# Attention in a hybrid decoder layer: the products of the turned probabilities with the values wait for both heads' copies

## The chip, the cores and the metric

The kernel runs on one core of one Trainium2 chip. The time is in device microseconds. Before the change three runs took 1358.27, 1357.81 and 1360.36 us; their median is 1358.27 us.

## The reference

One decoder layer on 1024 tokens of width 1024, all in float32. Cut to the part around the change:

```
q, k, v, iq, ik, iw, hq, hf, hi, hg = split(x @ w_in)
score = sum_h iw[t,h] * relu(iq[t,h] . ik[s])            # indexer, causal
keep the 256 best keys of each query                      # mask
s   = (q . k) * 64**-0.5, -inf where not kept             # 8 heads of 64
att = softmax(s) @ v
hgo = hgrn2(hq, hf, hi, hg)                                # 4 heads of 128, chunkwise
x   = LayerNorm(alpha * x + concat(att, hgo) @ w_o)
x   = LayerNorm(alpha * x + relu(x @ w_up)**2 @ w_down)
```

## The kernel before, in words

The layer is one program in stages: input projections with the choice of keys and the recurrent heads beside them, then attention, then the output projection with `w_o`, the first layer norm, and the two products of the feed-forward part. A scheduler of the language sets the order on each engine: it takes the instructions in the order in which the code issues them, with their dependencies, and lets an instruction go ahead of others on its engine by an estimate of when it is ready. So the written order is a wish, and the built order is read from the program.

Attention works on four pairs of heads (`hp`). Queries come in eight tiles of 128 (`t`), taken two at a time (`m` = 0, 2, 1, 3). For one query tile `scores` (L667) makes the products of queries and keys (L684, L685, in two parts of the keys) into one of four PSUM banks; VectorE adds the mask and takes the row maximum (L686), GpSimd scales it (L688), and ScalarE takes the exponent (L690) into the tiles `pr` or `prs`.

The probabilities have to be turned before they can meet the values. A unit of that is (`hp`, `m`, `c`): two query tiles, and the two key tiles 2c and 2c+1. `turn` (L694) does it for each of the two heads: four transposes on TensorE (L703; three where `c == m`, on the diagonal, since one of the four blocks is masked) into a PSUM bank of the tag `tr`, of which there are two, and a copy into `pt`: by VectorE for head 0, by ScalarE for head 1 (L710 and L712). `gather` (L715) makes the products with the values. A full unit (`c < m`) has four of them, head 0 and 1 for each of two key tiles, 256 columns each (L729). Head 0 writes the partitions 0 to 63 of the result, head 1 the partitions 64 to 127, so the page shows them as `128*64`: 128 rows by 64 columns of the array. A unit on the diagonal has two products of 128 columns (L731) and two of 256; the one at `m == 0` has six of 128 (L726, L727). There are ten units in a pair of heads and 40 in all.

The loop over `plan` (L763) issues the scores of a query tile and, between them, the turns of the pair of tiles before; the products run `LAG = 2` units behind the turns (L782). `normalise` (L741) closes half a pair: products with `ident` that spread the reciprocal sums (L744), a copy, a multiplication and the split into two parts.

`fetch` (L650) loads queries, keys and values of the next pair; the loads of the keys (`ks`) are issued only when an exponent of the pair before is done (L662). The four key loads of a head are two parts of the keys, each written twice, and L685 uses the second part. `w_o` follows: its weights are split into two parts (L88 on ScalarE, L89 on GpSimd) once the last exponent is done (L873), and its products (L123 to L125) fill the gaps in the last part of attention.

Of the kernel before, what the change touches and what calls it, by code (L numbers as in the profile page):

```python
# [13 lines left out]
AF = mybir.ActivationFunctionType  # L14
# [28 lines left out]
def layer(ctx, tc, x, w_in, w_o, lb_logits, hg_norm_g, ln1_g, ln1_b, w_up, w_down, ln2_g, ln2_b,  # L43
          rope_tab, turn_tab, ident_c, causal_c, level_c, block_c, out, probe=None):
    nc = tc.nc
    PE, ACT, DVE, POOL = nc.tensor, nc.scalar, nc.vector, nc.gpsimd
# [27 lines left out]
    def tr_bank(shape=(P, 4, P)):  # L74
        return bank("tr", 2, shape)

    def ou_bank(shape=(P, 512)):
        return bank("ou", 2, shape)
# [7 lines left out]
    def split_out(hi, lo, src, eng=None):  # L86

        first = ACT.activation(hi, src, AF.Copy)  # L88
        (eng or DVE).tensor_tensor(lo, src, hi.bitcast(F32), op=OP.subtract)  # L89
        return first  # L90

    def behind(a, b):
        tc.add_manual_dep(a.ins, b.ins.name, mybir.DependencyInfo(
            mybir.DependencyClass.Sync, mybir.DependencyReason.DATA), reason="order of the work")
# [496 lines left out]
    for at in range(1, 29):  # L591
        if at in groups:
            g = groups[at]()
# [50 lines left out]
    bp = es_b.enter_context(tc.tile_pool(name="bp", bufs=1, reuse_waits="tile"))  # L644
    scale = HD ** -0.5
    PB = 5, 4
    PT, LAG, FT = 8, 2, 1
    pairs, probs, parts = {}, {}, {}

    def fetch(hp, after=None):  # L650

        qs = bq.tile([P, 2, S], F32R, name="qs1") if hp % 2 else qp.tile([P, 2, S], F32R, name="qs")
        for j in range(2):
            dma(qs[j * HD:(j + 1) * HD].bitcast(F32), qd[j, 2 * hp:2 * hp + 2].rearrange("h x d s -> (x d) h s"))
        ks = []
        for hh in range(2):
            ks.append([wp.tile([P, S], F32R, name="ks", tag="w", bufs=9) for _ in range(2)])
            for j in range(2):
                for r in range(2):
                    d = dma(ks[hh][j][r * HD:(r + 1) * HD].bitcast(F32), kd[j, 2 * hp + hh].rearrange("x d s -> (x d) s"))  # L660
                    if after is not None:
                        behind(d, after)  # L662
        va = bq.tile([P, NT, P], F32, name="va1") if hp % 2 else bp.tile([P, NT, P], F32, name="va")
        dma(va, vd[:, hp * P:(hp + 1) * P].rearrange("(t p) n -> p t n", p=P))
        pairs[hp] = {"ks": ks, "qs": qs, "va": va}

    def scores(hp, t):  # L667
        ks, qs = pairs[hp]["ks"], pairs[hp]["qs"]
        W = P * (t + 1)
        mask = causal[:, P:] if t == 0 else causal if t == 1 else score[t - 2]  # L670
        cuts = 1 if W <= 512 else 2
        n = W // cuts
        if "sums" not in pairs[hp]:
            pairs[hp]["sums"] = bp.tile([P, NT, 2], F32, name="sums", bufs=2)
        sums = pairs[hp]["sums"][:, t]
        mx = bp.tile([P, 2, 2], F32, name="mx", bufs=4)
        nm = bp.tile([P, 2], F32, name="nm", bufs=4)
        pr = [bp.tile([P, S], F32, name="pr", bufs=PB[0]) if t > 3 else bp.tile([P, 512], F32, name="prs", bufs=PB[1])
              for _ in range(2)]
        for hh in range(2):  # L680
            for ci in range(cuts):
                c = slice(ci * n, (ci + 1) * n)
                ps = mm_bank()
                PE.matmul(ps[:, :n], qs[:, hh, t * P:(t + 1) * P], ks[hh][0][:, c], start=True, stop=False)  # L684
                PE.matmul(ps[:, :n], qs[:, hh, t * P:(t + 1) * P], ks[hh][1][:, c], start=False, stop=True)  # L685
                DVE.tensor_tensor_reduce(pr[hh][:, c], ps[:, :n], mask[:, c], 1.0, mx[:, 0, hh:hh + 1] if ci else -HUGE,  # L686
                                         op0=OP.add, op1=OP.max, accum_out=mx[:, ci, hh:hh + 1])
        POOL.tensor_scalar(nm, mx[:, cuts - 1], -scale, None, op0=OP.mult)  # L688
        for hh in range(2):
            pairs[hp]["last"] = ACT.activation(pr[hh][:, :W], pr[hh][:, :W], AF.Exp, bias=nm[:, hh:hh + 1],  # L690
                                               scale=scale, accum_out=sums[:, hh:hh + 1])
        probs[hp, t] = pr

    def turn(hp, m, c):  # L694

        parts[hp, m, c] = []
        for hh in range(2):
            pt = bp.tile([P, 2, 2, P], F32, name="pt", bufs=PT)
            tp = tr_bank((P, 2, 2, P))
            n = 4 if c < m else 3  # L700
            for i in range(2):
                for g in range(2 * c, 2 * c + 2 if c < m or i else 2 * c + 1):
                    PE.transpose(tp[:, g % 2, i], probs[hp, 2 * m + i][hh][:, g * P:(g + 1) * P], ident)  # L703
            if c < m:
                cp = [(pt.rearrange("p g t n -> p (g t n)"), tp.rearrange("p g t n -> p (g t n)"))]
            else:
                cp = [(pt[:, 0], tp[:, 0]), (pt[:, 1, 1], tp[:, 1, 1])]
            for d, u in cp:
                if hh:
                    ACT.activation(d, u, AF.Copy)  # L710
                else:
                    DVE.tensor_copy(d, u)  # L712
            parts[hp, m, c].append(pt)

    def gather(n, hp, m, c):  # L715
        half, i = divmod(2 * m, 4)
        if c == 0 and i == 0:
            pairs[hp]["o", half] = ou_bank((P, 4, P))
        o, va, pt = pairs[hp]["o", half], pairs[hp]["va"], parts.pop((hp, m, c))
        for g in (0, 1) if c < m else (1, 0):  # L720
            for hh in range(2):
                sl = slice(hh * HD, (hh + 1) * HD)
                lhs = va[:, 2 * c + g, sl]
                if m == 0:
                    if g == 1:
                        PE.matmul(o[sl, i], va[:, 0, sl], pt[hh][:, 0, 0], start=True, stop=True)  # L726
                    PE.matmul(o[sl, i + 1], lhs, pt[hh][:, g, 1], start=g == 1, stop=g == 0)  # L727
                elif c < m or g == 0:
                    PE.matmul(o[sl, i:i + 2], lhs, pt[hh][:, g], start=c == 0 and g == 0, stop=c == m)  # L729
                else:  # L730
                    PE.matmul(o[sl, i + 1], lhs, pt[hh][:, 1, 1], start=False, stop=False)  # L731
        if c == m and i == 2:
            sums = pairs[hp]["sums"][:, 4 * half:4 * half + 4]
            wide = bq.tile([P, 4, 2, HD], F32, name="wide")
            DVE.reciprocal(sums, sums)
            POOL.tensor_copy(wide, sums.unsqueeze(3).to_broadcast([P, 4, 2, HD]))
            late.append((n, hp, half, o, wide))

    late = []

    def normalise(due, hp, half, o, wide):  # L741
        ps = tr_bank()
        for i in range(4):
            PE.matmul(ps[:, i], wide[:, i].rearrange("p h d -> p (h d)"), ident, start=True, stop=True)  # L744
        r = bq.tile([P, 4, P], F32, name="recip")
        ACT.activation(r, ps, AF.Copy)
        DVE.tensor_tensor(r, o, r, op=OP.mult)
        split_out(MH[half][:, :, hp, :], ML[half][:, :, hp, :], r, POOL)
# [9 lines left out]
    turned_ = [p for p in plan if p[0] == "turn"]  # L758
    fetch(0)
    hgt = turn_hg()  # L760
    next(g1)
    nt = ns = 0
    for n, (kind, hp, *u) in enumerate(plan):  # L763
        if kind == "scores":
            scores(hp, *u)
            if ns < 4:
                next(hgt)
                next(hgt)
            if ns < 2:
                next(g1)  # L770
            if ns == 4:
                for _ in hgt:
                    pass
                es_h.close()
                bq = es_b.enter_context(tc.tile_pool(name="bq", bufs=1, reuse_waits="tile", side="right"))
            if (ns == 4 or ns > 8 and u[0] == FT) and hp < 3:
                fetch(hp + 1, pairs[hp]["last"])
            ns += 1
        else:
            turn(hp, *u)  # L780
            nt += 1
            if nt > LAG:  # L782
                gather(nt, *turned_[nt - 1 - LAG][1:])
                if late and late[0][0] + 2 <= nt:
                    normalise(*late.pop(0))
    for p in turned_[nt - LAG:]:
        gather(nt, *p[1:])
    for u in late:
        normalise(*u)
# [372 lines left out]
```

## Time and profile before

| | |
|---|---|
| median of three runs | 1358.27 us |
| the profiled execution: time, span of its instructions | 1360.36 us, 1358.1 us |
| PE (TensorE matmul) busy | 1308.9 us, 96% |
| DVE (VectorE), ACT (ScalarE), POOL (GpSimd) busy | 71%, 44%, 28% |
| attention, from the first to the last transpose of probabilities | 464.7 to 605.2 us |
| products with the values (L726 to L731) | to 611 us |

The trace counts two instructions for one product with the values: a run "x8" of L729 is four products. A transpose is counted once. A run is a row of equal instructions; its length is read as the time from its start to the start of the next row, since the pipeline lets the ends overlap. "PEld" is the load of the stationary operand.

### The profile page before, as it was taken

The page shows a single profiled execution, that of the slowest core. Times are in us where ns is not written, and L with a number is a line of the kernel's source. Part 1 is how long each engine was busy: PE and PEld are TensorE (multiplying, and loading weights), DVE is VectorE, ACT ScalarE, POOL GpSimd, SP SyncE. Part 2 cuts the span into 40 slices and gives each one's busy share as a digit, 9 for nine tenths or more (in the row PEclk, how much of TensorE's full clock was granted, in tenths as well). Part 3 has the DMA queues.
Part 4 walks back from the last instruction along what each step waited for, and adds up shares of the span by engine and source line. Part 5 has one row for each costly group of instructions (what it writes and reads, how often), then busy time and mean ns, then how long its engine had stood idle before and what let it go on. Part 6 is the DMA issues. An engine that isn't in the chain of part 4 may idle for free.

```text
span 1358.1 us, 21018 instructions
## 1 busy us (share of the span) xinstructions
PE 1308.9 (96%) x8007; PEld 1065.7 (78%) x8007; DVE 960.5 (71%) x1731; ACT 599.0 (44%) x1070; POOL 375.1 (28%) x374
## 2 busy tenths in 40 slices
PE   9999999799989999999989999999998999999996
PEld 8888788687879866668867888888886788888875
DVE  5576579999998555523487666656628999887478
ACT  3442457555432655542235555555544343333131
POOL 3452523535253111143480000000005342231016
PEclk9999999899999999999999999999999999999999
DMA  6333411202013564035223544444467555352223
GB/s 231 103 118 106 133 53 32 64 2 64 33 56 75 138 147 109 1 117 166 106 78 106 189 135 152 148 163 147 141 215 275 181 165 185 118 163 92 80 76 124
DMA packets 93620, 162.50 MB, mean 120 GB/s; under 512 B 6600, under 2 KB 37712, under 8 KB 93392
## 3 DMA queue, kind: packets, MB, share of 16 engines
q1 hardware_dynamic: 72880, 122.89, 28.9%
q10 hardware_dynamic: 20640, 38.28, 8.1%
q8 instruction: 63, 1.03, 0.3%
q14 instruction: 37, 0.30, 0.1%
HBM read 114.48 MB, written 46.66 MB: 119 GB/s over the span
## 4 chain that ended last, share of the span: by engine, by line
PE 67%; DVE 18%; DMA 6%; POOL 4%; issue 3%; ACT 1%; SPq 0%; DVEq 0%; POOLq 0%; ACTq 0%
PE ps L124 18%; PE ps L123 18%; PE ps L125 18%; DVE junk L322 6%; PE ps L729 3%; PE ps L703 3%; DMA qd<-rparts 2%; DMA kd<-rparts 2%; PE ps L684 2%; DVE hgk L492 1%; PE ps L685 1%; DVE hgq L491 1%; POOL tn L904 1%; POOL acc L830 1%; DVE pos L380 1%
## 5 line engine op out<-in xcount | busy, mean ns | idle before, releaser
L125 PE MATMUL ps<-w,xt 128*128 128x512 f32 (+2 forms) x448 | 157.7, 353 | 0.0
L124 PE MATMUL ps<-w,xt 128*128 128x512 f32 (+2 forms) x448 | 156.9, 352 | 0.0
L123 PE MATMUL ps<-tw,sh 128*128 128x512 f32 x392 | 152.8, 393 | 4.2 <-DVE acc L1068 2.4
L123 PE MATMUL ps<-w,xt 128*128 128x512 f32 (+2 forms) x448 | 156.0, 354 | 0.5 <-ACT xt L88 0.5
L124 PE MATMUL ps<-tw,sh 128*128 128x512 f32 x392 | 154.4, 394 | 1.9 <-DVE tw L89 1.9
L125 PE MATMUL ps<-tw,sh 128*128 128x512 f32 x392 | 153.1, 393 | 0.4 <-DVE sh L89 0.4
L89 POOL TENSOR_TENSOR w<-wraw,w 128x512 fp32r<-128x512 f32 (+1 forms) x76 | 102.4, 1368 | 108.8 <-ACT w L88 78.4
L1048 POOL TENSOR_TENSOR tt<-rb,rb 128x1536 f32<-128x1536 f32 (+1 forms) x5 | 18.4, 3677 | 390.9 <-PE ps L125 314.1
L1070 DVE TENSOR_TENSOR acc<-acc,ps 128x512 f32<-128x512 f32 x140 | 92.0, 678 | 35.4 <-PE ps L125 35.2
L88 ACT ACTIVATE sh<-rs 128x1536 fp32r<-128x1536 f32 (+1 forms) x35 | 49.1, 1403 | 151.7 <-PE ps L125 140.8
L123 PE MATMUL ps<-xt,w 128*128 128x512 f32 x256 | 102.9, 402 | 0.0
L322 DVE TENSOR_SCALAR_CACHE_REDUCE junk<-score,cand 128x384 uint8<-128x384 f32 (+1 forms) x124 | 100.4, 810 | 3.0
L125 PE MATMUL ps<-xt,w 128*128 128x512 f32 x256 | 102.2, 402 | 0.0
L124 PE MATMUL ps<-xt,w 128*128 128x512 f32 x256 | 101.8, 398 | 0.0
L124 PE MATMUL ps<-xt,wq 128*128 128x512 f32 x256 | 99.9, 390 | 0.0
L123 PE MATMUL ps<-xt,wq 128*128 128x512 f32 x256 | 99.7, 389 | 0.0
L125 PE MATMUL ps<-xt,wq 128*128 128x512 f32 x256 | 99.5, 390 | 0.0
L340 ACT ACTIVATE sjunk<-score,cand 128x896 int8<-128x896 f32 (+1 forms) x62 | 67.9, 1095 | 66.6 <-DVE cand L351 64.0
L123 PEld LDWEIGHTS ps<-w,xt 128*128 128x128 f32 x448 | 84.7, 190 | 11.6 <-ACT xt L88 1.0
L124 PEld LDWEIGHTS ps<-w,xt 128*128 128x128 f32 x448 | 84.9, 190 | 11.2 <-issue 1.3
L125 PEld LDWEIGHTS ps<-w,xt 128*128 128x128 f32 x448 | 85.0, 190 | 10.5 <-issue 0.4
L123 PEld LDWEIGHTS ps<-tw,sh 128*128 128x128 f32 x392 | 74.0, 189 | 20.8 <-DVE acc L1068 2.8
(242 smaller groups left out, 3063.6 us busy)
## 6 DMA issues: line engine op xcount, KB each, us to landing
hs<-h ACTq DMA_DIRECT2D x98, 256.0 KB
rs<-hs SPq DMA_DIRECT2D x28, 768.0 KB
wr<-in_w_up_dram SPq DMA_DIRECT2D x16, 1024.0 KB
rb<-in_w_down_dram SPq DMA_DIRECT2D x16, 768.0 KB
wraw<-in_w_in_dram SPq DMA_DIRECT2D x40, 256.0 KB
ks<-kd SPq DMA_DIRECT2D x32, 256.0 KB
xn<-in_x_dram SPq DMA_DIRECT2D x8, 512.0 KB
kd<-rparts ACTq DMA_DIRECT2D x16, 256.0 KB
```

What stands on the lines that cost most here:

```text
L88: first = ACT.activation(hi, src, AF.Copy)
L89: (eng or DVE).tensor_tensor(lo, src, hi.bitcast(F32), op=OP.subtract)
L123: PE.matmul(ps, ah, bh, start=first, stop=False, **kw)
L124: PE.matmul(ps, ah, bl, start=False, stop=False, **kw)
L125: return PE.matmul(ps, al, bh, start=False, stop=last, **kw)
L322: DVE.tensor_scalar(junk[:, :wide[j]], score[j], at, 0.0, op0=op, op1=OP.add, accum_out=res)
L340: ACT.activation(sjunk[:, :wide[j]], score[j], AF.Sign, bias=0.0 if at is None else at[:, j:j + 1], scale=1.0, accum_out=cnt[:, j:j + 1])
L684: PE.matmul(ps[:, :n], qs[:, hh, t * P:(t + 1) * P], ks[hh][0][:, c], start=True, stop=False)
L703: PE.transpose(tp[:, g % 2, i], probs[hp, 2 * m + i][hh][:, g * P:(g + 1) * P], ident)
L729: PE.matmul(o[sl, i:i + 2], lhs, pt[hh][:, g], start=c == 0 and g == 0, stop=c == m)
L1048: POOL.tensor_tensor(t1, b12, b11, op=OP.subtract)
L1070: DVE.tensor_tensor(acc[t][:, gs], acc[t][:, gs], ps, op=OP.add)
```

## The change

The copies of a unit are noted by head, and the first product of the unit gets a dependency on both of them, where it had one on its own head's copy alone. `BATCH = 1` gives one unit at a time. `normalise` is issued before the products of the step instead of behind them.

```
-    PT, LAG, FT = 8, 2, 1
-    pairs, probs, parts = {}, {}, {}
+    PT, LAG, BATCH, FT = 8, 2, 1, 1
+    pairs, probs, parts, copies, waited = {}, {}, {}, {}, []
...
-                if hh:
-                    ACT.activation(d, u, AF.Copy)
-                else:
-                    DVE.tensor_copy(d, u)
+                copy = ACT.activation(d, u, AF.Copy) if hh else DVE.tensor_copy(d, u)
+                copies[hp, m, c, hh] = copy
...
+    def values(r):
+
+        while waited:
+            behind(r, waited.pop())
...
-                    PE.matmul(o[sl, i:i + 2], lhs, pt[hh][:, g], start=c == 0 and g == 0, stop=c == m)
+                    values(PE.matmul(o[sl, i:i + 2], lhs, pt[hh][:, g], start=c == 0 and g == 0, stop=c == m))
...
-            if nt > LAG:
-                gather(nt, *turned_[nt - 1 - LAG][1:])
-                if late and late[0][0] + 2 <= nt:
-                    normalise(*late.pop(0))
-    for p in turned_[nt - LAG:]:
+            if late and late[0][0] + 2 <= nt:
+                normalise(*late.pop(0))
+            if nt - LAG - gathered >= BATCH:
+                batch = turned_[gathered:nt - LAG]
+                waited += [copies[(*p[1:], hh)] for p in batch for hh in range(2)]
+                for p in batch:
+                    gather(nt, *p[1:])
+                gathered += len(batch)
+    for p in turned_[gathered:]:
         gather(nt, *p[1:])
```

`values` wraps the other first products (L726, L731) in the same way. The new lines move the numbers: L729, L731, L744 and L747 of the kernel before are L732, L734, L747 and L750 of the changed one, and L726 and L727 are L729 and L730.

On TensorE, in the second pair of heads, the three full units of `m == 3` that have no scores between them (`ident` marks transposes, `pt,va` products with the values) stood so:

```order
L703 MATMUL ps<-ident,pr 128x128 x4
L729 MATMUL ps<-pt,va_5270 64x256
L703 MATMUL ps<-ident,pr 128x128 x4
L729 MATMUL ps<-pt,va_5270 64x256 x3
L703 MATMUL ps<-ident,pr 128x128 x4
L729 MATMUL ps<-pt,va_5270 64x256
L703 MATMUL ps<-ident,pr 128x128 x4
L729 MATMUL ps<-pt,va_5270 64x256 x3
L703 MATMUL ps<-ident,pr 128x128 x3
L729 MATMUL ps<-pt,va_5270 64x256
L703 MATMUL ps<-ident,pr 128x128 x3
L729 MATMUL ps<-pt,va_5270 64x256 x3
```

One product of a unit stood between the transposes of the two heads, and three behind them. On the same engine, at the same place, the changed program has:

```order
L703 MATMUL ps<-ident,pr 128x128 x8
L732 MATMUL ps<-pt,va_5270 64x256 x4
L703 MATMUL ps<-ident,pr 128x128 x8
L732 MATMUL ps<-pt,va_5270 64x256 x4
L703 MATMUL ps<-ident,pr 128x128 x6
L732 MATMUL ps<-pt,va_5270 64x256 x4
```

The single product has moved behind the second head's transposes and stands with the other three; the transposes of both heads stand together.

On TensorE, at the first scores of the second pair, with the semaphores that each instruction waits for (`DMAHW` are DMA queues; `qs_5255` is the second pair's queries), the kernel before has:

```order
L703 MATMUL ps<-ident,prs 128x128 [waits DVE_49]
L703 MATMUL ps<-ident,prs 128x128 x2
L729 MATMUL ps<-pt,va 64x256
L685 MATMUL ps<-ks,qs_5255 128x128 [waits DMAHW3_49,DMAHW2_49]
L684 MATMUL ps<-ks,qs_5255 128x256 [waits DVE_49]
L685 MATMUL ps<-ks,qs_5255 128x256
L703 MATMUL ps<-ident,prs 128x128 [waits Activation_49]
L703 MATMUL ps<-ident,prs 128x128 x2
L729 MATMUL ps<-pt,va 64x256 x3
```

On the same engine the changed program has there:

```order
L685 MATMUL ps<-ks,qs_5255 128x128 [waits DMAHW3_49,DMAHW2_49]
L703 MATMUL ps<-ident,prs 128x128 [waits DVE_49]
L703 MATMUL ps<-ident,prs 128x128 x2
L703 MATMUL ps<-ident,prs 128x128 [waits Activation_49]
L703 MATMUL ps<-ident,prs 128x128 x2
L732 MATMUL ps<-pt,va 64x256 x4
L684 MATMUL ps<-ks,qs_5255 128x256 [waits DVE_49]
L685 MATMUL ps<-ks,qs_5255 128x256
```

The product L685 that waits for two key loads now stands ahead of both heads' transposes and of all four products of the unit, where three transposes and a product stood ahead of it before.

## Rows read from the trace of the kernel before

**Rows 1.** Page, busy time by engine; and the chain that ended last, by engine

```profile
PE 1308.9 (96%) x8007; PEld 1065.7 (78%) x8007; DVE 960.5 (71%) x1731; ACT 599.0 (44%) x1070; POOL 375.1 (28%) x374
...
PE 67%; DVE 18%; DMA 6%; POOL 4%; issue 3%; ACT 1%; SPq 0%; DVEq 0%; POOLq 0%; ACTq 0%
```

**Rows 2.** Windows, one pair period: us, busy by engine, PE clock, DMA share, GB/s

```profile
497.26:531.40 34.14, 33.81 (x223) 23.74 (x222) 20.17 (x66) 20.29 (x51) 5.40 (x12) 1.00 0.46 109
```

**Rows 3.** Waits of PE from 460 to 625: total us, times, longest

```profile
PE ps L703 <- ACT pt L710: 1.0, 3, 0.3
PE ps L703 <- DVE pt L712: 0.5, 1, 0.5
```

**Rows 4.** Timeline of PE, second pair: start us, us, instruction xcount

```profile
526.08 0.65 PE L729 MATMUL ps<-pt,va 128*64 128x256 f32 x2
526.66 0.66 PE L703 MATMUL ps<-ident,pr 128*128 128x128 f32 x4
527.24 1.08 PE L729 MATMUL ps<-pt,va 128*64 128x256 f32 x6
528.25 0.55 PE L703 MATMUL ps<-ident,pr 128*128 128x128 f32 x3
```

**Rows 5.** Timeline of PE, last pair

```profile
587.15 0.88 PE L703 MATMUL ps<-ident,pr 128*128 128x128 f32 x6
587.96 0.32 PE L731 MATMUL ps<-pt,va 128*64 128x128 f32 x1
587.96 0.43 PE L729 MATMUL ps<-pt,va 128*64 128x256 f32 x1
...
596.05 1.08 PE L729 MATMUL ps<-pt,va 128*64 128x256 f32 x8
597.07 0.50 PE L124 MATMUL ps<-w,xt 128*128 128x512 f32 x1
```

**Rows 6.** Tile pt, its weight loads: ns min/median/max, first and last start

```profile
L729 PEld LDWEIGHTS ps<-pt,va x240: 132/137/138, 472.1 to 610.2; 128*64 128x64 f32 x120
```

**Rows 7.** Timeline of PE, a lone product of 128 columns

```profile
566.36 0.43 PE L731 MATMUL ps<-pt,va 128*64 128x128 f32 x2
566.73 0.44 PE L684 MATMUL ps<-ks,qs 128*128 128x384 f32 x1
```

**Rows 8.** Timeline of PE, four transposes with scores behind them

```profile
545.35 0.60 PE L703 MATMUL ps<-ident,prs 128*128 128x128 f32 x4
...
545.70 0.48 PE L684 MATMUL ps<-ks,qs 128*128 128x512 f32 x1
```

**Rows 9.** Timeline of SP, PEld and PE: the second pair's keys

```profile
470.49 4.93 SPq L49 DMA_DIRECT2D ks<-kd  x8
...
482.36 0.19 PEld L685 LDWEIGHTS ps<-ks,qs 128*128 128x128 f32 x1 [0.41 <-issue]
...
484.25 0.42 PE L684 MATMUL ps<-ks,qs 128*128 128x320 f32 x1
```

**Rows 10.** Windows, while those keys load

```profile
476.00:480.00 4.00, 4.00 (x25) 2.52 (x26) 3.52 (x10) 2.71 (x6) 0.21 (x1) 1.00 1.03 222
```

**Rows 11.** Timeline of DVE and ACT, copies of a unit, with the idle time before

```profile
526.19 0.69 DVE L712 COPY pt<-ps 128x512 f32<-128x512 f32 x1 [2.06 <-PE ps L703]
...
527.35 0.60 ACT L710 ACTIVATE pt<-ps 128x512 f32<-128x512 f32 x1 [2.16 <-PE ps L703]
```

**Rows 12.** Timeline of ACT, the last exponent and the copy behind it

```profile
585.33 1.13 ACT L690 ACTIVATE pr<-pr,nm 128x1024 f32<-128x1024 f32 x1
...
586.46 0.52 ACT L710 ACTIVATE pt<-ps 128x256 f32<-128x256 f32 x2
```

**Rows 13.** Timeline of PE, a pause later in the span

```profile
1057.66 0.67 PE L123 MATMUL ps<-tw,sh 128*128 128x512 f32 x1 [2.38 <-DVE acc L1068]
```

**Rows 14.** Windows, behind that pause

```profile
1057.70:1061.20 3.50, 3.50 (x9) 2.74 (x10) 3.50 (x3) 0.68 (x1) 2.64 (x1) 0.52 0.74 227
```

**Rows 15.** Windows of 2 us, second pair: one in which VectorE is full

```profile
545.40:547.40 2.00, 2.00 (x18) 1.83 (x16) 2.00 (x8) 0.86 (x2) 0.79 (x2) 1.00 0.00 0
```

More of the change, by code (lines that the diff above doesn't have):

```diff
@@ L725, in gather @@
                     if g == 1:
-                        PE.matmul(o[sl, i], va[:, 0, sl], pt[hh][:, 0, 0], start=True, stop=True)
+                        values(PE.matmul(o[sl, i], va[:, 0, sl], pt[hh][:, 0, 0], start=True, stop=True))
                     PE.matmul(o[sl, i + 1], lhs, pt[hh][:, g, 1], start=g == 1, stop=g == 0)
                 elif c < m or g == 0:
-                    PE.matmul(o[sl, i:i + 2], lhs, pt[hh][:, g], start=c == 0 and g == 0, stop=c == m)
+                    values(PE.matmul(o[sl, i:i + 2], lhs, pt[hh][:, g], start=c == 0 and g == 0, stop=c == m))
                 else:
-                    PE.matmul(o[sl, i + 1], lhs, pt[hh][:, 1, 1], start=False, stop=False)
+                    values(PE.matmul(o[sl, i + 1], lhs, pt[hh][:, 1, 1], start=False, stop=False))
         if c == m and i == 2:
@@ L761, in layer @@
     next(g1)
-    nt = ns = 0
+    nt = ns = gathered = 0
     for n, (kind, hp, *u) in enumerate(plan):
```

## The prediction

> **What bounds the kernel now.** I read the page first. TensorE is busy for 96% of the span, and the chain that ended last runs over it for 67% [rows 1]. Then the windows over attention: in one pair of heads, 34.14 us long, PE is busy for 33.81 us, VectorE and ScalarE for about 20 each, and the clock is at its full share [rows 2]. The list of waits says the same from the other side: from 460 to 625 us PE waited 1.5 us for copies, all told [rows 3]. So this stage is as long as PE's instructions are, in the order in which they stand, and the question is what the order costs. That is read from the timeline, where the length of a run is the time from its start to the start of the next.
>
> A lone product of 256 columns between transposes takes 0.58 us (526.08 to 526.66); the other three products of the unit take 1.01 (527.24 to 528.25) [rows 4]. Once in the trace all four stand together: 596.05 to 597.07, 1.02 us [rows 5]. Three cost what four cost. The reason is in the same group: a product of head 0 and one of head 1 start at the same 587.96, since each uses 64 columns of the array. A pair costs what one product costs. So a run costs about 0.13 us, and 0.44 for each pair or lone product of 256 columns (1.01 less 0.58 is one step), half of that for 128 columns. This gives 0.57, 1.01 and 1.01 for one, three and four products, and 0.35 for a lone one of 128 columns, where the row has 0.37 [rows 7].
>
> Transposes pay for the change of form too. Four between products take 0.58 us (526.66 to 527.24) [rows 4]; six take 0.81 [rows 5], so one more costs 0.11 and eight come to 1.03, not 1.16. Four with scores behind them take 0.35 [rows 8].
>
> **The change, part by part.** The unit "4 transposes, 1 product, 4 transposes, 3 products" takes 0.58 + 0.58 + 0.58 + 1.01 = 2.75 us [rows 4]; "8 transposes, 4 products" comes to 1.03 + 1.02 = 2.05. That is 0.7 less, and the order shows it for most of the 40 units. Counted over TensorE's order:
>
> Lone products of 256 columns: 17 before, 2 now; 15 x 0.58 = 8.7 us. Lone products of L731: 9 before, 1 now; 8 x 0.36 = 2.9. Runs of three (14) and four (1) become 2 and 13, at no cost. The units at `m == 0` stood in three runs, 0.36 + 0.58 + 0.58 by the step prices, and stand in one, 0.13 + 6 x 0.11 = 0.79: 0.73 for each of three pairs and 0.36 for the first, whose unit stood in two runs, so 2.5 us. Products: 14.1 us.
>
> Transposes: 78 runs become 62. Sixteen joined runs at 0.15 are 2.4 us. Steps from a transpose to a product fall by 21, five more than that; at those five, scores now follow, which by the rows of four is up to 0.2 each, 0.9 us. Transposes: 3.3 us. Score runs fall from 50 to 45, each maybe 0.1 cheaper or not at all; I count nothing. Sum without new waits: 17.4 us.
>
> The added wait itself I price at nothing where the order is as shown: in the changed order the first product of a unit follows transposes of the next units, and these already waited for the same copies, since there are only two `tr` banks. What stands queued behind the waiting product are the other products, the next transposes and the scores; the copies and the row maxima would wait for those. In the tight stretch a copy on VectorE takes 0.69 us after 2.06 of idleness, and one on ScalarE 0.60 after 2.16 [rows 11]. The unit shrinks by 0.7, so the idleness stays above 1.3 and covers both.
>
> Here a rule of the Trainium skill speaks against the change. The row first: a weight load of such a product takes 137 ns [rows 6], and eight of them, 1.1 us, would be longer than the 1.02 us that the run of four takes [rows 5], so they overlap with products there. The Trainium skill's page "TensorE: Matmul & The Clock Gate", section "Part 3: Packing small matmuls — row/col tiling", says that loads overlap with matmuls in flight only where the row groups differ, and the two heads here use the same 128 rows. By the rule four products together would take some 2 us and the sum would be the transposes' 3.3 alone; by the row it is 17.4. I go by the row.
>
> **What is given back.** At the second pair's first scores the order moves PE towards a DMA. The keys are issued at 470.49 in eight loads [rows 9], behind an exponent ahead of which PE gains 0.5 us at most, and the queues are full at 222 GB/s while they land [rows 10]. L685 needs the last two; its weight load sits idle for 0.41 us, ended by no engine, and starts at 482.36 [rows 9]. So the kernel before arrives there just in time. The new order arrives earlier and waits: up to 482.36 it should have won about 0.5 (the first unit, with its transposes) + 0.75 (three units behind it, one lone product fewer) + 0.5 (a diagonal unit) and it has moved three transposes and a lone product, 1.05, behind that point, some 2.8 us of idle time. Behind it the kernel before needs 1.9 us to the scores at 484.25 [rows 9]; the new one has L685, 0.14, six transposes, 0.8, four products, 1.02, and scores of 256 columns, 0.3: 2.3. It is 0.4 late there, and the 2.5 us of the sum that lie up to this point (1.75 and 0.7 for this unit) are gone: 2.9 us back. The loads don't get faster with PE, so I take it in full. From there on the gain runs again.
>
> At the end of attention the last exponents stand on ScalarE, and a copy follows at 586.46 for 0.52 us [rows 12]. The second head's transposes need the bank that this copy frees; the new order gets there before it, about half a microsecond. Of the rest, `w_o` starts from the last exponent in both kernels. 17.4 - 2.9 - 0.5 = 14.0 us.
>
> The profiled execution took 1360.36 us, 2.1 above the median, with a span of 1358.1; 14.0 less is 1346.4 against it, and against the median 1344.3 us. What I can't price: the 2.8 us pause may let the clock fall. Later in the span a pause of 2.38 us [rows 13] is followed by 3.5 us at a share of 0.52, the lower level of 1.2 GHz, in which nine products run [rows 14]. At half speed such a stretch would cost up to 1.8 us here; at best nothing. Stretches in which VectorE is full (in five of the pair's 17 windows of 2 us, as in [rows 15]) could hold back what is saved inside them, up to 1.5 us a pair, 6 us in all, at best nothing.
>
> **Rivals.** First, no gate: if the keys land earlier, or the wait is shorter than worked out, the whole 17.4 us come, 1340.9 us. For it: the stall is worked out, not seen. Against it: the idle row before the load.
>
> Second, the copies become the bound. With half of the products' gain lost to waits for copies and row maxima, 14.0 - 7 gives 1351.3 us. For it: the full stretches of VectorE [rows 15]. Against it: 1.5 us of such waits now, and engines that idle for 2 us before such a copy [rows 3, 11]. The Trainium skill warns of it in "TensorEngine Tiling (Array Packing)", section "Performance Considerations": a faster TensorE leaves the copies out of PSUM as the bottleneck. In this stretch the rows have idle copies.
>
> Third, slower: the joined wait stalls PE's queue. Head 1's copy stands on ScalarE behind exponents of up to 1.13 us [rows 12]. If each of the 34 product runs waited 0.6 us for it, 20 us would be lost, 1365 us; it decides from 14.0 / 34 = 0.41 us a run. Against it: two units of lag, and transposes ahead of the products that already waited.
>
> Fourth, the change doesn't do what it says: the heads' products don't run side by side when their loads stand together, as by the rule above. Then only the transposes' part is left and the gate takes most of it: 1358 us, no change. Against it: the run of four at the price of two pairs, and the two starts at 587.96 [rows 5].
>
> **How the numbers follow.** Forecast 0.66 (1342 to 1347.5 us), no gate 0.12, copies 0.15, joined wait 0.04, no effect 0.03. The range goes from the rival without the gate, with the score runs, 1340.5, to the middle of the copies' case, 1351: about 0.1 is left out above it. A measurement of this kernel tells 0.2%, 2.7 us, from no change. Forecast, no gate and copies are all faster: 0.93; the last rival is no change: 0.03; the joined wait is slower: 0.04.
>
> **What would show it.** Runs of four products at about 1.02 us and runs of eight transposes at 1.03 in the second to fourth pair; a pair period of 29.4 to 30 us instead of 34.14; PE idle for 2 to 3 us before L685 at 482.4, at the same time as before; no stage behind attention changed in length. I am wrong if runs of four take near 2 us, if PE's waits for copies rise above 5 us, or if L685 of the second pair starts well before 482.

## The result: 12.5 us less, with most steps at the size that was worked out

The changed kernel took 1346.34, 1346.75 and 1348.60 us. A fourth run, at 1809.39 us with a mean granted clock of 0.654, was disturbed and is in no comparison, and neither is one of 1956.78 us in a later repeat. The ratio to the kernel before is 0.9908, 95% interval [0.9895, 0.9921]: 0.92%, 12.5 us; the medians by themselves, 1358.28 and 1346.75 us, lie 11.5 apart. That is faster, clear of no change, and inside the range; the forecast stood at 1344.3. A repeat gave 0.9906 [0.9888, 0.9925].

The two profiled executions, 1360.36 and 1346.34 us, lie 14.0 apart. Of that 0.8 us lies ahead of attention, where the change has no part: the first scores start at 444.81 before and at 444.00 after. All differences below are counted from there.

The page first, and the windows over one pair period (from one normalising product to the same one of the next pair), which answer to [rows 1, 2] (busy time of PE, PEld, DVE, ACT and POOL, then the granted clock, DMA share and GB/s):

```profile
PE 1289.3 (96%) x8007; PEld 1058.6 (79%) x8007; DVE 959.0 (71%) x1731; ACT 597.6 (44%) x1070; POOL 378.2 (28%) x374
...
493.74:523.75 30.01, 29.18 (x222) 22.29 (x222) 20.05 (x69) 19.79 (x50) 5.47 (x12) 1.00 0.51 119
```

TensorE has the same 8007 instructions and is busy 19.6 us less. The pair period fell from 34.14 to 30.01 us, while VectorE and ScalarE are as busy in it as they were, some 20 us each. PE's idle time in it rose from 0.33 to 0.83 us.

The timeline of PE in the second pair answers to [rows 4, 5]:

```profile
487.45 1.04 PE L703 MATMUL ps<-ident,pr 128*128 128x128 f32 x8
488.42 1.08 PE L732 MATMUL ps<-pt,va 128*64 128x256 f32 x8
489.44 1.09 PE L703 MATMUL ps<-ident,pr 128*128 128x128 f32 x8
490.46 1.08 PE L732 MATMUL ps<-pt,va 128*64 128x256 f32 x8
```

Each product of 256 columns has two records, so x8 is the run of four. From start to start: eight transposes 0.97 behind scores and 1.02 behind products, four products 1.02.

The second pair's keys [rows 9], on SP, PEld and PE:

```profile
469.68 4.93 SPq L49 DMA_DIRECT2D ks<-kd  x8
...
481.41 0.19 PEld L685 LDWEIGHTS ps<-ks,qs 128*128 128x128 f32 x1 [1.86 <-issue]
...
479.49 0.28 PE L685 MATMUL ps<-ks,qs 128*128 128x256 f32 x1
481.44 0.30 PE L685 MATMUL ps<-ks,qs 128*128 128x128 f32 x1 [1.68 <-DMA ks<-kd]
481.58 0.84 PE L703 MATMUL ps<-ident,prs 128*128 128x128 f32 x6
482.35 1.08 PE L732 MATMUL ps<-pt,va 128*64 128x256 f32 x8
```

This is the predicted pause: the idle time before the weight load has gone from 0.41 to 1.86 us, and the load starts at 481.41, as far behind the issue of the keys (11.7 us) as before (11.9). The waits of PE from 460 to 610 us (total us, times, longest) answer to [rows 3]; L709 holds both copies, L710 and L712 of the kernel before:

```profile
PE ps L703 <- ACT pt L709: 2.3, 5, 0.7
PE ps L685 <- DMA ks<-kd: 1.7, 1, 1.7
PE ps L703 <- DVE pt L709: 1.3, 4, 0.4
PE ps L684 <- DMA ks<-kd: 0.2, 1, 0.2
```

Waits for copies went from 1.5 to 3.6 us, 2.1 more, of which the prediction had 0.5.

The whole account, from the first scores to the start of the last product. Each instruction of PE is counted from its start to the next start without the idle time, and this is summed by kind; idle times of over 0.1 us stand apart:

| us | before | after | difference | predicted |
|---|---|---|---|---|
| products | 51.00 | 37.03 | -13.97 | -14.1 |
| transposes | 37.96 | 35.24 | -2.72 | -3.3 |
| scores | 40.77 | 40.66 | -0.11 | 0 |
| normalising, weights of other stages | 34.31 | 33.22 | -1.09 | not priced |
| waits for copies | 1.44 | 3.61 | +2.17 | +0.5 |
| wait for the keys | 0 | 1.89 | +1.89 | +2.9 |
| small rest | 0.12 | 0.30 | +0.18 | |
| sum (first scores to last product) | 165.60 | 151.95 | -13.65 | -14.0 |

Some 0.5 us of the unpriced row may only have moved: from the last product to the end of the span the kernel before takes 747.69 us and the changed one 748.16. So from the first scores to the end of the span the changed kernel is 13.2 us shorter.

### The profile page after: what moved, and what is told of

Read it like the earlier page. It is cut to its first block, busy times and chain, and to the rows that moved or that the text cites. A ratio compares the mean times of both kernels' runs of the same rounds, so it can differ in the third digit from the quotient of the medians.

```text
span 1344.1 us, 21007 instructions
## 1 busy us (share of the span) xinstructions
PE 1289.3 (96%) x8007; PEld 1058.6 (79%) x8007; DVE 959.0 (71%) x1731; ACT 597.6 (44%) x1070; POOL 378.2 (28%) x374
## 3 DMA queue, kind: packets, MB, share of 16 engines
q8 instruction: 63, 1.03, 0.3%
## 4 chain that ended last, share of the span: by engine, by line
PE 62%; DVE 21%; DMA 8%; POOL 3%; issue 3%; ACT 2%; SPq 1%; DVEq 0%; ACTq 0%; POOLq 0%
PE ps L124 18%; PE ps L125 18%; PE ps L123 18%; DVE junk L322 8%; DMA qd<-rparts 3%; PE ps L703 2%; DVE hgk L492 2%; PE ps L732 2%; DMA kd<-rparts 2%; DVE hgq L491 1%; PE ps L684 1%; POOL tn L911 1%; PE ps L685 1%; POOL acc L837 1%; DVE thr L354 1%
## 5 line engine op out<-in xcount | busy, mean ns | idle before, releaser
L124 PEld LDWEIGHTS ps<-w,xt 128*128 128x128 f32 x448 | 85.0, 190 | 11.9 <-issue 1.5
```

Of the source, the lines that this page charges most:

```text
L124: PE.matmul(ps, ah, bl, start=False, stop=False, **kw)
```

## Experiments

Each was timed against the kernel before. Two of the change's three edits needed no run. The earlier normalising by itself leaves the order of every engine as it was before, and the added wait by itself gives the order of the changed kernel, on all engines. The added wait is the change.

**Do neighbours have to belong to different heads?** (unpair)

```diff
-        for g in (0, 1) if c < m else (1, 0):
-            for hh in range(2):
+        for hh in range(2):
+            for g in (0, 1) if c < m else (1, 0):
```

> The changed kernel with the two loops of the products swapped, so that a unit's two products of one head stand next to each other, and not those of two heads; the joined wait stays. Theory A (two neighbouring products of different heads run side by side, two of one head do not): a run of four goes from 1.015 us to about 1.44 (three slots of 0.43 instead of two), the 8 runs with two 128-wide products from 0.80 to about 1.2, the four m==0 runs by some 0.2 each; 13 x 0.43 + 8 x 0.43 + 4 x 0.2 + 3 long runs x 0.43 = about 11 us slower than the changed kernel, less up to 1.9 us that the pause for the second pair's keys hides: 1356 to 1358 us. Theory B (the gain comes only from fewer changes between transposes, products and scores, whichever head the neighbours belong to): a run of four stays at about 1.02 us, the time at 1346 to 1348 us.

1348.09 us, ratio 0.9925 [0.9913, 0.9938]. Theory A, which is the prediction's own picture of pairs, falls: the run of four takes 1.02 us in this order too. The timeline of PE shows why, in a unit whose products stand in the order head 0 of 128 columns, head 0 of 256, head 1 of 128, head 1 of 256:

```profile
488.85 0.45 PE L734 MATMUL ps<-pt,va 128*64 128x128 f32 x4
489.12 0.61 PE L732 MATMUL ps<-pt,va 128*64 128x256 f32 x4
```

Rows stand by their start, and both products of 128 columns (four records) start ahead of any of 256. So head 1's product, third in the program, has started before head 0's second: it doesn't wait for its turn. Of the whole units only those of `m == 0`, with three products of each head in a row, got dearer, 1.07 us in place of 0.81. Two units at the end of attention whose products stand in two runs, now one run for each head, got dearer by 0.43 us each. The time does not tell this kernel from the changed one: the two intervals overlap.

The profiled execution of this kernel, 1351.59 us, also ran at the lower clock behind the pause, 0.58 of full speed, and nowhere else in attention. Windows:

```profile
480.00:484.00 4.00, 2.82 (x13) 2.15 (x15) 1.47 (x8) 2.96 (x9) 0.21 (x1) 0.58 1.02 229
484.00:490.00 6.00, 6.00 (x34) 4.57 (x33) 2.30 (x8) 2.13 (x8) 0.21 (x1) 0.71 0.30 69
```

**Do the heads run side by side at all?** The time of the last kernel could also mean that nothing does, and that a run just costs a fixed amount and a price for each product. So the same edit was made in the kernel before, without the joined wait, where it turns runs of 1 + 3 products into runs of 2 + 2 of one head each (split_heads).

> The kernel before (no added wait) with the loops of the products swapped: the first run of a unit holds both products of head 0, the second both of head 1, where before it was one product and three. The number of runs and of changes of form is the same (64 runs of products), only the split is 2 + 2 and not 1 + 3. Theory C (a run takes 0.16 us and 0.43 for each product of 256 columns of the head that has more of them, since the two heads run side by side and two products of one head do not): 1.02 + 1.02 in place of 0.58 + 1.01 in some 15 units, 0.80 + 0.80 in place of 0.36 + 0.79 in some 9, about 0.2 more in each m == 0 unit: about 11 us slower than before, 1369 to 1371 us. Theory E (nothing runs side by side; a run costs a fixed 0.36 us and 0.21 for each product): 0.79 + 0.79, the same sum as 0.58 + 1.01: no change, 1357 to 1360 us.

1374.22 us, ratio 1.0109 [1.0092, 1.0127]: slower by 14.6 us. PE's timeline:

```profile
525.71 1.08 PE L729 MATMUL ps<-pt,va 128*64 128x256 f32 x4
526.71 0.66 PE L703 MATMUL ps<-ident,pr 128*128 128x128 f32 x4
527.30 1.08 PE L729 MATMUL ps<-pt,va 128*64 128x256 f32 x4
528.31 0.66 PE L703 MATMUL ps<-ident,pr 128*128 128x128 f32 x4
```

Two products of one head (x4 records) take 1.01 us, as long as the two of each head above. Theory C's prices hold, theory E falls. The products sum to 62.81 us against 51.00 before (+11.8) in the account's terms, and up to the last product the kernel is 12.1 us longer. That the time lies 3 us above theory C's range comes from behind the last product, 2.7 us, where PE waits 2.5 us more for VectorE's `acc` (L1068) than in the kernel before; why was not followed. A run lasts as long as the head that has more of it.

**How far apart may they stand?** Products of two units in one run, all of head 0 ahead of all of head 1 (heads_apart), against the same runs with the heads in turn (l1_b2_keys, below).

```diff
-                for p in batch:
-                    gather(nt, *p[1:])
+                for hh in range(2):
+                    for p in batch:
+                        gather(nt, *p[1:], (hh,))
```

> As l1_b2_keys (products of two units in one run), but in each run all products of head 0 stand first and then all of head 1. It asks how far apart the two heads' products may stand and still run side by side. Theory F (a head has one product running and one waiting; a third one holds up what is behind it): in a run of eight products of 256 columns the second head starts when the first head's second product is done, 0.16 + 2 x 0.43 + 4 x 0.43 = 2.7 us, and runs of six of 256 and two of 128 take about 2.5 us; over 15 such runs some 12 to 14 us slower than l1_b2_keys, about 1357 us. Theory G (they run side by side at any distance within a run): 1.88 and 1.67 us as in l1_b2_keys, 1343 to 1345 us. Theory H (only neighbours of different heads run side by side): 0.16 + 7 x 0.43 = 3.2 us and about 2.9, some 20 us slower.

1358.80 us, ratio 0.9990 [0.9980, 1.0000], 15.0 above l1_b2_keys; the two were not timed side by side, but the account has the same, 50.56 us of products against 35.41. PE's timeline has the run of eight products in l1_b2_keys, then, of this kernel, the start of a run with two products of 128 columns, and the run of eight:

```profile
486.86 1.95 PE L732 MATMUL ps<-pt,va 128*64 128x256 f32 x16
488.73 0.94 PE L747 MATMUL ps<-ident,wide 128*128 128x128 f32 x6
```

```profile
483.25 1.08 PE L732 MATMUL ps<-pt,va 128*64 128x256 f32 x4
484.16 0.27 PE L734 MATMUL ps<-pt,va 128*64 128x128 f32 x1
484.17 0.43 PE L732 MATMUL ps<-pt,va 128*64 128x256 f32 x1
484.27 0.27 PE L734 MATMUL ps<-pt,va 128*64 128x128 f32 x1
484.38 0.86 PE L732 MATMUL ps<-pt,va 128*64 128x256 f32 x5
...
488.29 2.86 PE L732 MATMUL ps<-pt,va 128*64 128x256 f32 x16
491.08 0.60 PE L747 MATMUL ps<-ident,wide 128*128 128x128 f32 x3
```

1.87 us against 2.79, where theory F said 2.7 and 2.5 for the other form, which took 2.58. In the first five rows here head 0 has two products of 256, one of 128 and one of 256. Its first two run alone, 0.92 us, and only as the third starts, at 484.16, does head 1's first product start beside it, at 484.17. So head 1 starts while one product of head 0 still waits, and not while two do.

**Does each half of the wait save by itself?** The wait only off the diagonal, and only on it.

```diff
-                waited += [... for p in batch for hh in range(2)]
+                waited += [... for p in batch for hh in range(2) if p[3] < p[2]]    (wait_full)
+                waited += [... for p in batch for hh in range(2) if p[3] == p[2]]   (wait_diag)
```

> The changed kernel with the added wait only on units off the diagonal (two 256-wide products of each head). Theory A (each joined run saves by itself: its lone products go, its transposes join): from the run prices 11.3 us less of TensorE's work than the kernel before, less some 1.5 to 3 us at the gate of the second pair's keys: 1349 to 1351 us. Rival (the gain comes only when all runs are joined, since the lone product of a diagonal unit keeps the changes of form): nearer to 1354 us than to 1350.

> The changed kernel with the added wait only on the diagonal units (those with 128-wide products, m==0 among them). Theory A: from the run prices 6.7 us less of TensorE's work than the kernel before, less 0.5 to 1.5 us at the gate: 1352 to 1353 us, and the gains of this one and of the kernel with the wait off the diagonal add up to that of the changed kernel within 2 us. Rival (joining needs both): about 1357 us.

wait_full: 1353.41 us, 0.9959 [0.9946, 0.9971], worse than expected. wait_diag: 1351.94 us, 0.9950 [0.9937, 0.9964], as expected. The gains, 0.41% and 0.50%, add up to the 0.92% of the whole within their intervals, so each half saves without the other. In wait_full 7.7 us of products went, in wait_diag 5.8. What wait_full gives back is on PE's timeline at the keys, and in a window:

```profile
479.96 0.34 PE L685 MATMUL ps<-ks,qs 128*128 128x128 f32 x1 [1.54 <-DMA ks<-kd]
480.10 1.51 PE L703 MATMUL ps<-ident,prs 128*128 128x128 f32 x6
481.53 1.98 PE L732 MATMUL ps<-pt,va 128*64 128x256 f32 x8
```

```profile
480.00:484.00 4.00, 4.00 (x19) 2.53 (x20) 1.49 (x9) 2.83 (x10) 0.21 (x1) 0.57 1.03 226
```

Behind the pause six transposes take 1.43 us in place of 0.77 and four products 1.91 in place of 1.02, at the lower clock of 1.2 GHz: 1.55 us. The pause itself, 1.54, was in the expectation; the clock and 1.3 us more of waits for copies were not. In the profiled execution they make 2.9 of the 3.4 us by which the time lies above the middle of theory A's range. The part behind the last product is also 1.6 us longer than in the kernel before; it ranges from 745.9 to 750.4 us over the profiles of all these kernels, and why was not followed.

**The gate.** The second pair's keys don't wait for the first pair's exponent (keys_early), and the same edit in the kernel before (before_keys).

```diff
-                    if after is not None:
+                    if after is not None and hp > 1:
                         behind(d, after)
```

> The changed kernel, but the second pair's eight key transfers do not wait for the exponent of the first pair, and so stand before the first pair's values and the six weight loads on the queue. Theory A (the 1.9 us of idle TensorE at the second pair's keys is what the gate gave back): the pause at 479 to 482 us goes, all later work of attention starts 1.5 to 1.9 us earlier, about 1345 us (0.11 to 0.14 % less than the changed kernel). Rival (the keys are bound by the DMA rate from 462 us on, 1.04 to 1.07 busy, whatever their place): the pause stays, no change. Second rival (the queue waits for a weight buffer at the earlier place and holds up the first pair's values and keys): a new wait ahead of the first pair, slower than 1348 us.

> The kernel before with the second pair's keys fetched early, as in keys_early. Theory (the gate costs only a TensorE that arrives early, so it is a price of the change, not of the kernel before): the 0.41 us of idle time at L685 goes and little more, 0.3 to 1 us faster than before, 1357.3 to 1358.6 us. Rival (the place of the keys is worth the same to both kernels, for instance by less traffic on the queues): 2 to 4 us faster, 1355 to 1356.5 us.

keys_early: 1343.67 us, 0.9886 [0.9873, 0.9900]. before_keys: 1358.76 us, 0.9993 [0.9984, 1.0001]. The timeline of keys_early, PE at the same place and SP:

```profile
478.63 0.82 PE L703 MATMUL ps<-ident,prs 128*128 128x128 f32 x6
479.38 1.08 PE L732 MATMUL ps<-pt,va 128*64 128x256 f32 x8
...
431.25 3.76 SPq L49 DMA_DIRECT2D ks<-kd  x6
...
454.67 3.64 SPq L49 DMA_DIRECT2D ks<-kd  x6
```

Two of the second pair's eight loads are the last of the row at 431.25, six are the row at 454.67, and the pause is gone. The account has 1.89 us less of waiting and 0.35 less of scores, 2.3 us in all to the last product and 1.7 to the end of the span. The kernel before got nothing that can be told from no change. So the late keys cost nothing until TensorE came early, and then some 2 us by the account: they are a price of the change. The times point the same way, but do not show it by themselves. The four of keys_early, 1342.67 to 1344.16 us, lie under all those of the changed kernel, yet they were not timed side by side, and the intervals of the two ratios overlap. With l1_b2_keys it is the fastest that was run.

**Does a pause always bring the clock down?** The changed kernel once more (after_again).

> The changed kernel once more, to set its time beside keys_early with more runs and to see whether the clock falls behind the pause at the second pair's keys. If the pause brings the clock down in some executions and not in others (as in the profiles of unpair and wait_full, and not in that of the changed kernel): times spread by some 2 us or more between 1346 and 1350, and a profile with a granted clock under 0.7 from 480 to 484 us is possible. If it never falls in this order of work: 1346 to 1348 us and the granted clock at 1.00 as before.

1346.20, 1346.87, 1347.60 and 1348.49 us, ratio 0.9906 [0.9888, 0.9925]. The same pause, 1.60 us, and a clock of 1.00 behind it. The last row is the same window of the changed kernel's first profile, behind its pause of 1.68 us:

```profile
481.28 0.30 PE L685 MATMUL ps<-ks,qs 128*128 128x128 f32 x1 [1.60 <-DMA ks<-kd]
...
480.00:484.00 4.00, 2.72 (x22) 2.05 (x22) 1.64 (x9) 3.50 (x10) 0.40 (x2) 1.00 0.88 210
480.00:484.00 4.00, 2.56 (x20) 1.89 (x20) 1.47 (x9) 3.46 (x9) 0.21 (x1) 1.00 0.99 217
```

Pauses of 1.54 and 1.71 us were followed by half speed, pauses of 1.60 and 1.68 were not. Times that spread by 2.3 us do not tell whether it falls in executions without a profile. What decides it stays open.

**Longer runs still.** Two units to a run, one unit of lag (l1_b2_keys), or three units of lag and ten buffers (l3_b2_keys), both with early keys.

```diff
-    PT, LAG, BATCH, FT = 8, 2, 1, 1
+    PT, LAG, BATCH, FT = 8, 1, 2, 1     (l1_b2_keys)
+    PT, LAG, BATCH, FT = 10, 3, 2, 1    (l3_b2_keys)
```

> The changed kernel with early keys, and with the products of two units gathered in one run after one unit of lag (26 runs of products, not 34). By the run prices 3.7 us less of TensorE's work in attention than the changed kernel, and no pause at the keys: about 1340 us. Rival (with one unit of lag the joined products come before the copies of the newer unit are done): 0.3 us of waiting at most of the 26 runs, some 6 to 8 us, slower than keys_early, 1346 us or more.

> As l1_b2_keys, with three units of lag and ten buffers for the turned probabilities (25 runs of products). By the run prices 2.4 us less of TensorE's work in attention than the changed kernel, no pause at the keys, and no wait for copies: about 1341.3 us. Rival (the scheduler's order puts the saved time back into scores and weights that wait for VectorE): 1343 to 1345 us, as keys_early.

l1_b2_keys: 1343.79 us, 0.9886 [0.9872, 0.9899]; l3_b2_keys: 1350.44 us, 0.9933 [0.9920, 0.9947]. Both expectations missed: the first gains nothing over keys_early, the second loses 6.8 us. In l1_b2_keys the products take 1.6 us less than in keys_early and the transposes 1.4, together 3.0 of the 3.7 that the run prices gave. The waits are 0.5 longer, the scores 0.9, the normalising products 0.7; some 0.7 us of where the rest went was not found. From the first scores to the end of the span it is 0.4 us shorter than keys_early, too little to tell them apart. PE's waits from 460 to 610 us, of keys_early and then of l3_b2_keys, and a window of the latter:

```profile
PE ps L703 <- ACT pt L709: 2.2, 5, 0.7
PE ps L703 <- DVE pt L709: 1.4, 4, 0.4
```

```profile
PE ps L703 <- DVE pt L709: 1.8, 4, 0.8
PE ps L747 <- DVE pt L709: 1.5, 3, 1.1
PE ps L703 <- ACT recip L749: 0.9, 1, 0.9
```

```profile
560.00:600.00 40.00, 37.07 (x220) 25.64 (x218) 13.24 (x37) 19.66 (x44) 15.55 (x16) 0.96 0.33 99
```

In l3_b2_keys the normalising products wait for copies, the clock of the last pair's window is no longer 1.00, and the scores sum to 43.5 us against 40.3. Why they are dearer was not followed further.

## Why the prediction was right, step by step

- **The bound.** TensorE's order set the length of the stage, and does still: the period fell by 4.13 us at the same busy time of VectorE and ScalarE.
- **Products, -14.1.** Measured -13.97. The prices 0.58, 1.01, 1.01 for one, three and four products came out to 0.01 us. The reason behind them was half right. That the heads run side by side is shown, by runs of two products of one head at 1.01 us. That neighbours pair off, one of each head, is not how it works; the run lasts as long as its fuller head. For the orders of this change both give the same number, so the price held by luck where the picture did not.
- **Transposes, -3.3.** Measured -2.72. Runs of eight between products take 1.02 where 1.03 was said. What is missing, 0.6 us, need not lie in the estimated part: a wait inside a run of transposes stretches the run by 0.16 us beside its idle time (0.27 from one start to the next in place of 0.11), and there are eight such waits, three of them of only 0.10, where there were four: 0.64 us.
- **The gate, +2.9.** The place and the instruction were right, the size was not: 1.89. Attention started 0.81 us earlier, and so did the keys' issue, so the deadline moved along. PE reached L685 at 479.76 (481.44 less 1.68). By the prediction it would have been at 482.36 - 2.8 - 0.8 = 478.8: the stretch up to there won 1.0 us less than worked out, 0.5 of it for waits of 0.31 and 0.21 us; where the other 0.5 went was not followed. So the sign that was named, 2 to 3 us of idle time, did not come: it is 1.68.
- **Waits at nothing, and 0.5 at the tail.** This is the mis-sized term: +2.17, and by two more pieces some 3.0. The small rest is three waits of 0.10 us for ScalarE's copies, and the stretched runs of transposes are the 0.64 above. The cover named, over 1.3 us of idle time on the copying engines, is there, but it covers the wrong thing. The timeline of PE, DVE and ACT in the second pair, units of `m == 2`:

```profile
502.34 0.60 PE L703 MATMUL ps<-ident,pr 128*128 128x128 f32 x4
502.70 0.48 PE L684 MATMUL ps<-ks,qs 128*128 128x512 f32 x1
503.02 0.40 PE L685 MATMUL ps<-ks,qs 128*128 128x512 f32 x1
503.73 0.98 PE L703 MATMUL ps<-ident,pr 128*128 128x128 f32 x7 [0.31 <-DVE pt L709]
505.13 0.55 PE L703 MATMUL ps<-ident,pr 128*128 128x128 f32 x3 [0.42 <-ACT pt L709]
...
502.98 0.69 DVE L709 COPY pt<-ps 128x512 f32<-128x512 f32 x1 [1.32 <-PE ps L703]
...
502.95 0.58 ACT L709 ACTIVATE pt<-ps 128x512 f32<-128x512 f32 x1
```

  The same transposes in the kernel before, also with two score products between them:

```profile
507.17 0.60 PE L703 MATMUL ps<-ident,pr 128*128 128x128 f32 x4
...
508.08 1.02 PE L703 MATMUL ps<-ident,pr 128*128 128x128 f32 x7
```

  VectorE had been idle for 1.32 us before its copy; what is late is the bank. The transposes at 502.34 are head 0's of a unit, and those at 503.73 begin with head 1's. Nothing was taken from between them, yet the kernel before has no wait here. In its built order the two heads write the two `tr` banks. In that of the changed kernel, in the second to fourth pair, both write the same bank, so head 1 waits for VectorE's copy, which starts when head 0's transposes are done and takes 0.69 us. The other bank was free hardly sooner: ScalarE's copy out of it ended at 503.53. These three waits are 0.9 of the 2.17. The waits of 0.10 us, the 0.31 in the first pair and the 0.69 at the tail stand where products that lay between two runs of transposes have moved away: they had been cover. No run was made with the banks given out another way, so what that would save is open. All the waits are 0.31 + 0.42 in each of three pairs, where 0.32 stood before; 0.31 in the first; 0.41 in the last, where 0.48 stood; and at the tail 0.69 where 0.5 was worked out.
- **Clock, up to 1.8.** Not in this profile; in two of the experiments it fell behind the same pause, for 1.55 us in one of them.
- **Rivals.** No gate: its 1340.9 us needed keys that land early, and with such keys the kernel came to 1343.7, with 3.6 us of waits for copies still there. Copies as the bound: 3.6 us of waits, under the 5 that would have shown it. Here belongs the warning of the Trainium skill's "TensorEngine Tiling (Array Packing)", section "Performance Considerations", that copies out of PSUM may become the bottleneck once tiling has made TensorE faster. Here they did not become the bound, but the waits for them grew by 2.2 us. Joined wait: no product waited for a copy; all waits stand at transposes. No effect: the run of four at 1.02 us.

In the account the misses nearly cancel, which is luck: waits +1.7, transposes +0.6, products and small rest +0.3 against gate -1.0, scores -0.1 and the unpriced rows -1.1, so 13.65 in place of 14.0. That the runs show 12.5 lies with the executions: the profiled one of the kernel before was the slowest of its runs, and that of the changed kernel the fastest.

## What to carry to other kernels

Where two column halves of TensorE's array have work, price a run by its fuller half, and collect the work of both before a change of form; the order inside a run matters little as long as neither half has more than two products standing ahead of the other's. After a gain, look at what the engine now reaches early: here late keys that had cost nothing took 2 us, and a one-line edit gave them back. A wait that is added to keep work together costs little if it stands behind other waits. But what lay between two users of a bank was cover, and it moves away with the work; and in the new order the banks may be given out anew. Look there for two users of one bank that stand close together: idle time on the copying engine does not cover them.

## What the runs showed of the hardware

- TensorE started a product ahead of one that stands before it in the program, where the two use different 64 columns: head 1's product of 128 columns, third in the built order of unpair, ahead of head 0's of 256, the second (both of 128 start before the first of 256 at 489.12). The Trainium skill's "TensorE: Matmul & The Clock Gate", section "Part 3: Packing small matmuls — row/col tiling", has matmuls start strictly in the order of the program. The trace does not agree, and it decides.
- That reach is short: with four products of one head ahead, the other head started 0.92 us late, with the third of them, and a run of eight took 2.79 us in place of 1.87.
- Two of one head ahead cost nothing (1.02 us for a run of four in unpair), three of 128 columns cost 0.26 us.
- In four profiles with a pause of 1.5 to 1.7 us at the same place, the clock behind it was 0.57, 0.58, 1.00 and 1.00.
